# Second MLP product: halves of the columns in the order 0, 1, 1, 0, with accumulators kept over two chunks

## The chip, the cores and the metric

The kernel runs on one core of one Trainium2 chip. The metric is the device time of one execution in microseconds (us). The core has a matrix engine (TensorE, in the profile PE, with its weight loads as PEld), a vector engine (VectorE, DVE), a scalar engine (ScalarE, ACT), GpSimd (POOL) and SyncE (SP), which issues the loads. Matmuls write into eight accumulator banks of 128 x 512 float32; only ACT and DVE read these.

## What is computed

The reference is one layer of an encoder on 256 tokens with 2048 features: two kinds of attention, a cross attention and an MLP, each followed by a LayerNorm. The change lies in the MLP:

```python
ff = jnp.square(jax.nn.relu(x @ w_mlp_in)) @ w_mlp_out      # 2048 -> 8192 -> 2048
x = layer_norm(ALPHA * x + ff, ln3_g, ln3_b)
```

## The kernel before

**Precision.** Every float32 product is made of three matmuls. Each operand is split into a high part (rounded to the matmul's format by a copy on ACT, L961) and a low part (operand minus high part, on DVE, L962); high x high, high x low and low x high are added in a bank (`mm3`, L163). A split of up to 1024 columns by 128 partitions is called a part here (`part`, L964). The high parts rotate through four buffers (`w_hi`), the low parts through four fixed ones.

**The MLP's loops.** The 8192 hidden features are four chunks of sixteen column tiles of 128. Two neighbouring tiles make a pair; a chunk has eight pairs, numbered 0 to 7. A column tile ("g", `hidden_tile`, L1027) multiplies 128 columns of the first weight by all 256 tokens: two parts, 32 matmuls. After its last matmul it is evacuated (L874: a copy on ACT, an add on DVE). Once both tiles of a pair are there, the pair's stages run (`stages`, L883): relu and square on ACT, the split of the square into high and low (`halve`), and, where it is asked for, four sums and differences of its blocks (`add`, three instructions on DVE) and their split (`halve_sums`).

A unit ("u") is one pair times one half of the output columns (1024 of 2048, `q` = 0 or 1), on one 1 MB tile of the second weight. A plain unit (P) takes eight block products, so 24 matmuls of 512 columns, and two parts. A unit in seven products (S, Strassen's scheme in Winograd's form) takes 21 matmuls, four parts, three adds on DVE for sums of weight blocks (`push_sums`, L948, into `s_t`), and the pair's own sums. It accumulates in seven banks: x11, x12, x21, and p1, p5, p6, p7; x22 gets plain units only, and serves as the bank of column tiles between S units.

**The order.** `items` (L914) lists tiles and units in the order of their work. A half-pass is eight units of one chunk and one half; tiles of the coming pairs stand between. Before, each half-pass has eight tiles (none in the last), its units go 0 to 7, pairs 0 to 5 as S and 6 and 7 as P; the last half-pass has P alone. With S and P for units and g for tiles, the first two half-passes read `ggSgSgSgSgSgSgPP gSgSgSgSgSgSgPgP`. At the end of every half-pass the banks are merged into the result rows `res` on DVE: eight operations of 512 columns for p1, p5, p6, p7 (L1153, handed out between parts through the deque `banks`) and four for the x banks (L1179). The last half-pass holds back the second token block of its last four units (`HELD`), to end with few matmuls.

**What is fixed in order.** Instructions passed through `queue` (L105) keep the order in which the program emits them on their engine: all splits, all matmuls of this stage, the weight sums, LN2's row adds (`norm_ops`, L1212). The pair stages are left to the scheduler, but those of a chunk's last pair (tile 15) and of the first four tiles go through `queue` too (L1063, L1056). A pair's stages are emitted at the next tile, or after the next unit, whichever comes first (L1073, L1176). `after(n, ...)` puts work behind the n-th coming part.

**Loads.** `fetch` (L925) issues one load of 1 MB per item, some three items ahead, into four tiles in turn; `row_b`, which first holds LN2's gain and bias rows, joins as the fifth at the item `JOIN` (L923). `norm_ops(0)` and `norm_ops(1)` apply these rows to the two column halves of `res`, four operations of 1024 columns each.

Of the kernel before, what the change touches and what calls it, by code (L numbers as in the profile page):

```python
# [38 lines left out]
def encoder_kernel(ctx: ExitStack, tc: tile.TileContext, t, out):  # L39
# [798 lines left out]
    ORDER = tuple(range(CH // 2))  # L838
    SEVENS = {cq: SEVEN for cq in PASSES[:-1]}
    SEVENS[PASSES[-1]] = ()  # L840
# [7 lines left out]
    ht_x = aux[:, 0:1024].rearrange("p (k c) -> p k c", c=512)  # L848
    sums_h = [aux[:, o:o + 1024] for o in range(1024, 8192, 1024)]
# [6 lines left out]
    place, free = {}, {"h": list(range(SLOTS)), "s": list(range(len(SEVEN) + 1))}  # L856

    def take(what, c, p):
        place[what, c, p] = free[what].pop(0)
# [23 lines left out]
    def stages(h, c, p, to=free_order):  # L883

        a11, a21, a12, a22 = [h[:, o:o + P] for o in range(0, 4 * P, P)]
        s = []

        def square():
            to(nc.scalar.activation(h, h, AF.Relu))
            to(nc.scalar.activation(h, h, AF.Square))  # L890

        def halve():
            take("h", c, p)
            x = hid(c, p)
            ordered_split(x[:, :, 0:S], x[:, :, S:2 * S], h.rearrange("p (i c) -> p i c", c=S), to)

        def add():
            s.append(tmp_tile())
            s3, s1, s2, s4 = [s[0][:, o:o + P] for o in range(0, 4 * P, P)]
            to(nc.vector.tensor_tensor(out=s[0][:, 0:2 * P].rearrange("p (i c) -> p i c", c=P),  # L900
                                       in0=a21[:, None, :].broadcast_to([P, 2, P]),
                                       in1=h.rearrange("p (i c) -> p i c", c=P)[:, 0:4:3, :], op=ALU.subtract))
            to(nc.vector.tensor_tensor(out=s2, in0=s1, in1=a11, op=ALU.subtract))
            to(nc.vector.tensor_tensor(out=s4, in0=a12, in1=s2, op=ALU.add))
# [10 lines left out]
    for c, q in PASSES:  # L915
        us = [("u", c, q, p) for p in ORDER]
        gs = [("g", c, j) for j in range(LEAD, CH)] if q == 0 else [
            ("g", c + 1, j) for j in range(LEAD) if c < NCH - 1]
        for u in us:
            n = 2 if q == 0 and u[3] == (CH // 2 - 2 if c else 0) else 1  # L920
            items += gs[:n] + [u]
            gs = gs[n:]
    JOIN = items.index(("u", 0, 1, 7))  # L923

    def fetch():  # L925

# [89 lines left out]
    def both(*todo):  # L1016
        return [lambda: [x() for x in todo]]

    now, late_finish, later, count = [], [], [], [0]

    def after(n, *todo):

        later.extend([(count[0] + n, x) for x in todo])
        later.sort(key=lambda x: x[0])


    def hidden_tile(it, ps):  # L1027
# [57 lines left out]
        x = sums_of(c, p)  # L1085
        return x[:, 0, i * P:(i + 1) * P], x[:, 1, i * P:(i + 1) * P]

    def one_pass(c, q):

        order, sevens = ORDER, SEVENS[c, q]  # L1090
        final = (c, q) == PASSES[-1]
# [3 lines left out]
        left = {id(ps): len(sevens) * (ps is not x22) + 2 * (len(order) - len(sevens)) for ps in xs}  # L1095
        left.update({id(ps): len(sevens) for ps in pt})
        left[id(x22)] -= 2 * HELD * final
        total = dict(left)
# [17 lines left out]
        def more(ps, op=ALU.add):  # L1116
            nc.vector.tensor_tensor(out=m_t, in0=m_t, in1=ps, op=op)

        spare, n_seven, n_unit, parts = [], 0, 0, []
        while n_unit < len(order):  # L1120
            it = step()
            if it[0] == "g":
                if n_unit == 0:
                    ps = {LEAD: x22, LEAD + 1: x21}[it[2]] if it[1] == 0 else p6
                elif n_seven < len(sevens):
                    ps = x22
                else:
                    spare = spare or [p1, p6]
                    ps = spare[0]
                    spare.reverse()  # L1130
                hidden_tile(it, ps)
                continue
            p, raw, k = it[3], raw_of[it], 2 * it[3]
            n_unit += 1
            if p in sevens:
                if n_seven == 0:
# [10 lines left out]
                n_seven += 1  # L1147
                if at[0] < len(items) and is_seven(items[at[0]]):
                    push_sums(items[at[0]])
                if n_seven == len(sevens):  # L1150
                    nc.scalar.activation(m_t, p1, AF.Copy)

                    banks.extend([lambda: merge(r11, m_t), lambda: more(p6),  # L1153
                                  lambda: merge(r12, m_t, ALU.subtract), lambda: more(p7, ALU.subtract),
                                  lambda: merge(r21, m_t), lambda: merge(r22, m_t, ALU.subtract),
                                  lambda: merge(r22, p5), lambda: merge(r12, p5)])
            elif final and len(order) - n_unit < HELD:
                n = len(parts) // 2
# [7 lines left out]
            else:  # L1166
                for i in range(2):
# [4 lines left out]
            if q == 1:  # L1172
                give("h", c, p)
                if p in SEVEN:
                    give("s", c, p)
            if late_finish:  # L1176
                late_finish.pop()()
        if not final:
            for r, ps in ((r22, x22), (r12, x12), (r11, x11), (r21, x21)):  # L1179
                merge(r, ps)  # L1180
            if c == NCH - 1:
                xs[:], pt[:] = pt[:], xs[:]
# [36 lines left out]
    for g in range(LEAD // G):  # L1219
# [163 lines left out]
```

## Time and profile before

| | |
|---|---|
| time, median of 3 runs | 1097.58 us (1096.8 to 1098.6) |
| the profiled execution's own time | 1098.32 us |
| its span, first to last instruction | 1096.5 us |
| granted TensorE clock, mean | 0.996 |
| first column tile of the MLP's stage | 446.1 us after the start |
| last matmul | 1085.2 us |

A row of the timeline gives start, length, engine, line of the program, operation, what it writes and reads, and in brackets how long the engine was idle before it and what ended the wait. A row of a group gives count, busy time, the mean of one in ns, and the idle time before. [...]

### The profile page before, as it was taken

What the parts mean: (1) busy time and instruction counts of PE and PEld (TensorE: products, weight loads), DVE (VectorE), ACT (ScalarE), POOL (GpSimd) and SP (SyncE); (2) the same over time, 40 slices, a digit from 0 to 9 for tenths busy, and PEclk for the clock granted to TensorE, in tenths of its full rate; (3) what the DMA queues carried; (4) which work ended last, traced back from release to release, by engine and by line L of the source; (5) the groups of instructions that cost most, each with busy time, mean ns of one, the idle gap of its engine ahead of it and who ended that gap; (6) DMA issues with size and microseconds to landing.
All of it is one profiled execution on the core that took longest, in us unless ns stands there. A gap on an engine that the chain in (4) does not pass through costs nothing.

```text
span 1096.5 us, 15253 instructions
## 1 busy us (share of the span) xinstructions
PE 1076.7 (98%) x5846; PEld 928.8 (85%) x5846; DVE 938.7 (86%) x1301; ACT 642.3 (59%) x937; POOL 36.2 (3%) x43
## 2 busy tenths in 40 slices
PE   9999999999999999999999999999999999999995
PEld 6988899988999878878888888888888888888885
DVE  6878678778889677999999999899999899999876
ACT  6555567555576426656566557466566566666640
POOL 2402000000000000000000000000000000000000
PEclk9999999999999999999999999999999999999998
DMA  9664454466577334555556555646556555655732
GB/s 327 246 227 136 156 189 157 156 228 238 182 216 267 143 128 176 209 192 198 191 202 244 202 188 199 216 170 226 198 186 225 198 192 198 224 175 195 253 145 78
DMA packets 37369, 215.87 MB, mean 197 GB/s; under 512 B 4272, under 2 KB 5168, under 8 KB 13616
## 3 DMA queue, kind: packets, MB, share of 16 engines
q1 hardware_dynamic: 37296, 214.89, 55.5%
q8 instruction: 46, 0.75, 0.3%
q14 instruction: 27, 0.22, 0.1%
HBM read 212.78 MB, written 2.10 MB: 196 GB/s over the span
## 4 chain that ended last, share of the span: by engine, by line
PE 92%; DVE 6%; issue 1%; ACT 1%; DMA 1%; SPq 0%; POOL 0%; DVEq 0%; ACTq 0%
PE acc L164 12%; PE acc L165 12%; PE acc L166 12%; PE acc L1035 11%; PE att L1035 6%; PE acc L1043 6%; PE att L165 5%; PE att L166 5%; PE att L164 5%; PE att L1043 3%; PE acc L206 2%; PE acc L204 2%; PE acc L205 2%; DVE lo L962 2%; PE acc L213 1%; PE att L213 1%
## 5 line engine op out<-in xcount | busy, mean ns | idle before, releaser
L87 ACT ACTIVATE w_hi<-raw 128x1024 fp32r<-128x1024 f32 (+2 forms) x134 | 131.6, 989 | 108.5 <-PE acc L166 73.9
L88 DVE TENSOR_TENSOR w_lo<-raw,w_hi 128x1024 fp32r<-128x1024 f32 (+2 forms) x130 | 147.2, 1142 | 50.3 <-ACT w_hi L87 49.2
L962 DVE TENSOR_TENSOR lo<-raw,w_hi 128x1024 fp32r<-128x1024 f32 (+1 forms) x156 | 173.0, 1128 | 9.2 <-ACT w_hi L961 9.0
L961 ACT ACTIVATE w_hi<-raw 128x1024 fp32r<-128x1024 f32 (+1 forms) x156 | 149.3, 980 | 25.5 <-PE acc L166 15.0
L1035 PE MATMUL acc<-x2t,w_hi 128*128 128x512 f32 x592 | 153.3, 391 | 0.0
L1035 PEld LDWEIGHTS acc<-x2t,w_hi 128*128 128x128 f32 x592 | 108.9, 189 | 19.6
L962 DVE TENSOR_TENSOR lo<-s_t,w_hi 128x1024 fp32r<-128x1024 f32 x84 | 102.4, 1222 | 10.8 <-ACT w_hi L961 10.7
L961 ACT ACTIVATE w_hi<-s_t 128x1024 fp32r<-128x1024 f32 x84 | 88.6, 1057 | 37.3 <-PE acc L1035 18.4
L1043 PEld LDWEIGHTS acc<-x2t,lo 128*128 128x128 f32 x592 | 80.8, 190 | 5.8
L1043 PE MATMUL acc<-x2t,lo 128*128 128x256 f32 x592 | 82.5, 282 | 0.0
L1035 PE MATMUL att<-x2t,w_hi 128*128 128x512 f32 x304 | 78.4, 391 | 0.0
L165 PE MATMUL acc<-lo,ht 128*128 128x512 f32 (+1 forms) x188 | 73.0, 389 | 1.1 <-DVE lo L962 1.1
L164 PE MATMUL acc<-w_hi,ht 128*128 128x512 f32 x186 | 72.5, 390 | 0.0
L166 PE MATMUL acc<-w_hi,ht 128*128 128x512 f32 x186 | 72.4, 389 | 0.0
L876 ACT ACTIVATE tmp<-acc 128x256 f32<-128x256 f32 x41 | 15.4, 384 | 92.2 <-PE acc L1035 87.9
L165 PE MATMUL acc<-w_lo,xt 128*128 128x512 f32 (+2 forms) x192 | 69.3, 362 | 0.0
L166 PE MATMUL acc<-w_hi,xt 128*128 128x512 f32 (+2 forms) x192 | 69.2, 361 | 0.0
L164 PE MATMUL acc<-w_hi,xt 128*128 128x512 f32 (+2 forms) x192 | 65.6, 361 | 1.2 <-ACT w_hi L87 1.2
L1035 PEld LDWEIGHTS att<-x2t,w_hi 128*128 128x128 f32 x304 | 55.8, 189 | 10.0
L962 DVE TENSOR_TENSOR lo<-raw_x,w_hi 128x1024 fp32r<-128x1024 f32 (+1 forms) x50 | 55.4, 1124 | 0.6 <-ACT w_hi L961 0.4
L165 PE MATMUL att<-lo,aux 128*128 128x512 f32 x139 | 54.4, 391 | 1.4 <-DVE lo L962 1.4
L164 PE MATMUL att<-w_hi,aux 128*128 128x512 f32 x139 | 54.1, 390 | 0.0
(287 smaller groups left out, 2513.1 us busy)
## 6 DMA issues: line engine op xcount, KB each, us to landing
raw<-in_w_mo SPq DMA_DIRECT2D x39, 1024.0 KB, 4.8
raw<-in_w_mc SPq DMA_DIRECT2D x37, 1024.0 KB, 4.8
raw<-in_w_out SPq DMA_DIRECT2D x16, 1024.0 KB, 4.9
raw_x<-in_w_mo SPq DMA_DIRECT2D x14, 1024.0 KB, 4.8
raw_x<-in_w_mc SPq DMA_DIRECT2D x12, 1024.0 KB, 4.8
row_b<-in_w_mo SPq DMA_DIRECT2D x11, 1024.0 KB, 4.8
raw<-in_w_mi SPq DMA_DIRECT2D x8, 1024.0 KB, 4.8
row_b<-in_w_mc SPq DMA_DIRECT2D x7, 1024.0 KB, 4.8
```

Of the source, the lines that this page charges most:

```text
L87: pin(nc.scalar.activation(hi, src, AF.Copy), pinned)
L88: return pin(nc.vector.tensor_tensor(out=lo, in0=src, in1=f(hi), op=ALU.subtract), pinned)
L164: keep(nc.tensor.matmul(ps, ah, bh, start=start, stop=False))
L165: keep(nc.tensor.matmul(ps, ah, bl, start=False, stop=False))
L166: keep(nc.tensor.matmul(ps, al, bh, start=False, stop=stop))
L204: nc.tensor.matmul(ps, hi, xt[:, k, 0:S], start=k == 0, stop=False)
L205: nc.tensor.matmul(ps, hi, xt[:, k, S:2 * S], start=False, stop=False)
L206: nc.tensor.matmul(ps, lo, xt[:, k, 0:S], start=False, stop=k == nk - 1)
L961: queue(nc.scalar.activation(hi, src, AF.Copy))
L962: queue(nc.vector.tensor_tensor(out=lo, in0=src, in1=f(hi), op=ALU.subtract))
L1035: queue(nc.tensor.matmul(ps, hi[:, k * P:(k + 1) * P], x2t[:, k0 + k, :], start=k0 + k == 0, stop=k0 + k == KT - 1))
L1043: queue(nc.tensor.matmul(ps[:, 0:S], lo[:, k * P:(k + 1) * P], x2t[:, k0 + k, 0:S], start=False, stop=False))
```

## The change

The half-passes take the column halves in the order 0, 1, 1, 0, 0, 1, 1, 0 over the four chunks. Where two neighbouring half-passes have the same half, the banks stay open over both, and are merged once. So there are five groups of half-passes: the first alone, three of two, the last alone. Which unit is S or P, in which order the pairs come and how many tiles stand before each unit is written out in three tables. Half-passes 2 to 6 have six and ten tiles in turn (the first has eight, the second ten, the last none). The last tile of a chunk now stands before the unit of pair 5; the plain pair 6 and pair 7 follow without tiles, pair 7 as S in the first three chunks. With the same letters the order is:

```
ggPggSgSgSgSgSPS  ggPggPgSgSgSgSgSgS
gSgSgSgSgSgSPS    ggPggSgSgSgSgSgSgS
gSgSgSgSgSgSPS    ggPggSgSgSgSgSgSgS
gSgSgSgSgSgSPP    PSPSPPPP
```

Pair 0 of the first chunk no longer needs sums. x22 is merged on its own after a run of P that an S follows. `norm_ops(1)` moves from the second half-pass into the first parts of the first one, `JOIN` to its unit of pair 4. The hidden pairs get eight slots instead of nine, the sums eight instead of seven. In the last half-pass the banks trade places in another order, and the four held units write their low parts into slots of sums that are no longer read.

```diff
-    SEVEN = (0, 1, 2, 3, 4, 5)
-    PASSES = [(c, q) for c in range(NCH) for q in range(2)]
-    SEVENS = {cq: SEVEN for cq in PASSES[:-1]}
-    SLOTS = CH // 2 + 1
+    PASSES = [(c, (n + c) % 2) for c in range(NCH) for n in range(2)]
+    UNITS = ["PSSSSSPS", "PPSSSSSS", "SSSSSSPS", "PSSSSSSS", "SSSSSSPS", "PSSSSSSS", "SSSSSSPP", "PSPSPPPP"]
+    ORDERS = [(0, 1, 2, 3, 4, 5, 6, 7), (0, 6, 1, 2, 3, 4, 5, 7), (0, 1, 2, 3, 4, 5, 6, 7), (6, 0, 1, 2, 3, 4, 5, 7),
+              (0, 1, 2, 3, 4, 5, 6, 7), (6, 0, 1, 2, 3, 4, 5, 7), (0, 1, 2, 3, 4, 5, 6, 7), (7, 0, 6, 1, 2, 3, 4, 5)]
+    TILES = ["22111100", "22111111", "11111100", "22111111", "11111100", "22111111", "11111100", "00000000"]
+    SEVENS = {cq: [p for p, x in zip(o, u) if x == "S"] for cq, o, u in zip(PASSES, ORDERS, UNITS)}
+    SUMS = [set(SEVENS[c, 0] + SEVENS[c, 1]) for c in range(NCH)]
...
-        return [square, halve] + [add, halve_sums] * (p in SEVEN)
+        return [square, halve] + [add, halve_sums] * (p in SUMS[c])
...
-    JOIN = items.index(("u", 0, 1, 7))
+    JOIN = items.index(("u", 0, 0, 4))
...
+        c, q = PASSES[n]
+        final, units, sevens = n == len(PASSES) - 1, UNITS[n], SEVENS[c, q]
+        opens = n == 0 or PASSES[n - 1][1] != q
+        closes = final or PASSES[n + 1][1] != q
...
+        def tile_bank(it):
+
+            before, later_ = items[:at[0] - 1], items[at[0]:]
+            units = [x for x in before if x[0] == "u"][-1:] + [x for x in later_ if x[0] == "u"][:1]
+            if all(is_seven(x) for x in units) or it[1:] == (0, LEAD):
+                return x22
+            ahead = later_[:next(i for i, x in enumerate(later_) if is_seven(x))]
+            return p1 if sum(x[0] == "g" for x in ahead) % 2 or n == len(PASSES) - 2 else p6
...
+                    xs_done = [lambda r=r, ps=ps: merge(r, ps) for r, ps in ((r12, x12), (r11, x11), (r21, x21))]
+                    banks.extend([lambda: merge(r11, m_t), lambda: more(p6)] + xs_done * (units[-1] == "S") + [
+                        lambda: merge(r22, p5), lambda: merge(r12, p5),
+                        lambda: merge(r12, m_t, ALU.subtract), lambda: more(p7, ALU.subtract),
+                        lambda: merge(r21, m_t), lambda: merge(r22, m_t, ALU.subtract)])
...
+                if not final and n_unit < len(units) and units[n_unit] == "S":
+                    banks.append(lambda: merge(r22, x22))
...
-    for cq in PASSES:
-        if cq == (0, 1):
-            for i, x in enumerate(norm_ops(1)):
-                after(6 * i + 8, x)
-        one_pass(*cq)
+    for i, x in enumerate(norm_ops(1)):
+        after(2 * i + 6, x)
+    for n in range(len(PASSES)):
+        one_pass(n)
```

More of the change, by code (lines that the diff above doesn't have):

```diff
@@ L847, in encoder_kernel @@
     aux = big.tile([P, 8192], F32R, tag="big", name="aux")
-    ht_x = aux[:, 0:1024].rearrange("p (k c) -> p k c", c=512)
-    sums_h = [aux[:, o:o + 1024] for o in range(1024, 8192, 1024)]
+    sums_h = [aux[:, o:o + 1024] for o in range(0, 8192, 1024)]
     fixed = [late.tile([P, 1024], F32R, name=f"lo{i}") for i in range(4)]
@@ L854, in encoder_kernel @@
     fixed_lo.extend(fixed)
-    place, free = {}, {"h": list(range(SLOTS)), "s": list(range(len(SEVEN) + 1))}
+    place, free = {}, {"h": list(range(CH // 2)), "s": list(range(len(sums_h)))}
     def take(what, c, p):
@@ L909, in halve_sums @@
             ordered_split(y[:, 0, :], y[:, 1, :], s[0], to)
-        return [square, halve] + [add, halve_sums] * (p in SEVEN)
+        return [square, halve] + [add, halve_sums] * (p in SUMS[c])
     raws, raw_of, fetched, sums = [raw_x], {}, [0], deque()
     items = []
[L915 to L922, printed above, removed]
-    JOIN = items.index(("u", 0, 1, 7))
+    tiles = [("g", c, j) for c in range(NCH) for j in range(CH)][LEAD:]
+    for (c, q), order, counts in zip(PASSES, ORDERS, TILES):
+        for p, n in zip(order, counts):
+            items += [tiles.pop(0) for _ in range(int(n))] + [("u", c, q, p)]
+    JOIN = items.index(("u", 0, 0, 4))
     def fetch():
@@ L1014, in hidden_group @@
         return [lambda i=i, h=h: empty(i, h) for i, h in pairs], todo
-    def both(*todo):
-        return [lambda: [x() for x in todo]]
-    now, late_finish, later, count = [], [], [], [0]
+    now, late_finish, later, count, held_lo = [], [], [], [0], []
     def after(n, *todo):
@@ L1051, in hidden_tile @@
         if first:
-            after(4, lambda: evacuate(ps, h, j % 2, queue))
+            after(3 if j in (LEAD, LEAD + 2) else 4, lambda: evacuate(ps, h, j % 2, queue))
         else:
@@ L1094, in one_pass @@
         (x11, x12, x21, x22), (p1, p5, p6, p7) = xs, pt
[L1095 to L1098, printed above, removed]
+        if opens:
+            cols = [slice((2 * q + i) * 512, (2 * q + i + 1) * 512) for i in range(2)]
+            r11, r12, r21, r22 = run["res"] = [res[b][:, cc] for b in range(NB) for cc in cols]
+            whole = units if closes else units + UNITS[n + 1]
+            n_s, n_p = whole.count("S"), whole.count("P")
+            run["left"] = {id(ps): n_s + 2 * n_p for ps in (x11, x12, x21)}
+            run["left"].update({id(ps): n_s for ps in pt})
+            run["left"][id(x22)] = 2 * (n_p - HELD) * final
+            run["total"] = dict(run["left"])
+            run["fresh"] = [r11, r12, r21, r22] if c == 0 else []
+            run["s"] = run["sevens"] = n_s
+        r11, r12, r21, r22 = run["res"]
+        left, total, fresh = run["left"], run["total"], run["fresh"]
         def mm(ps, x, hi, lo):
@@ L1103, in mm @@
             mm3(ps, *x, hi, lo, start, left[id(ps)] == 0, queue)
-        cols = [slice((2 * q + i) * 512, (2 * q + i + 1) * 512) for i in range(2)]
-        r11, r12, r21, r22 = [res[b][:, cc] for b in range(NB) for cc in cols]
-        fresh = [r11, r12, r21, r22] if c == 0 else []
         def merge(r, x, op=ALU.add):
@@ L1117, in more @@
             nc.vector.tensor_tensor(out=m_t, in0=m_t, in1=ps, op=op)
-        spare, n_seven, n_unit, parts = [], 0, 0, []
-        while n_unit < len(order):
+        def tile_bank(it):
[5 more added lines that the diff above has]
+            return p1 if sum(x[0] == "g" for x in ahead) % 2 or n == len(PASSES) - 2 else p6
+        n_unit, parts = 0, []
+        while n_unit < len(units):
             it = step()
             if it[0] == "g":
[L1123 to L1131, printed above, removed]
+                hidden_tile(it, tile_bank(it))
                 continue
@@ L1135, in one_pass @@
             if p in sevens:
-                if n_seven == 0:
+                if run["s"] == run["sevens"] and not final:
                     while banks:
@@ L1166, in one_pass @@
             else:
+                if left[id(x22)] == 0:
+                    rest = units[n_unit - 1:]
+                    left[id(x22)] = total[id(x22)] = 2 * (len(rest) - len(rest.lstrip("P")))
                 for i in range(2):
@@ L1178, in one_pass @@
         if not final:
[L1179 to L1182, printed above, removed]
+            if closes and units[-1] == "P":
+                for r, ps in ((r22, x22), (r12, x12), (r11, x11), (r21, x21)):
+                    merge(r, ps)
+            if n == len(PASSES) - 2:
+                xs[:], pt[:] = [p1, p6, p7, p5], [x11, x12, x21, x22]
                 banks.extend([lambda b=b, r=r: stats(sts[b], r)
                               for b, r in ((0, r11), (0, r12), (1, r21), (1, r22))])
+                used = [place["s", c, p] for p in SEVENS[PASSES[-1]]]
+                held_lo[:] = [i for i in range(len(sums_h)) if i not in used] + used
             return
@@ L1226, in encoder_kernel @@
             rows = norm_ops(0)
-            (a1, a2, a3, a4), (b1, b2, b3, b4) = first, second
-            side.extend(wait * 4 + empty + [a1, b1, a3, a2, a4, b3] + both(b2, rows[0])
-                        + both(b4, rows[1]) + rows[2:])
+            (a1, a2), (b1, b2, b3, b4) = first, second
+            side.extend(wait * 4 + empty + [a1, b1, a2, b3, b2, b4] + rows)
             s_in.split, s_in.beside = queued_split, 2
```

29 lines of the change are left out of this document (11 added, 18 removed).

## The prediction

> **What bounds the kernel now.** The page's first part and the chain of waits come first:
>
> ```profile
> PE 1076.7 (98%) x5846; PEld 928.8 (85%) x5846; DVE 938.7 (86%) x1301; ACT 642.3 (59%) x937; POOL 36.2 (3%) x43
> ...
> PE 92%; DVE 6%; issue 1%; ACT 1%; DMA 1%; SPq 0%; POOL 0%; DVEq 0%; ACTq 0%
> ```
>
> PE sets the time; DVE holds 6% of the chain. A busy PE isn't a PE at full pace, so I read the pace from the timeline of PE, by the first matmul (L1035) of column tiles. (S is a unit in seven products, P a plain one, g a column tile.)
>
> ```profile
> 598.77 1.98 PE L1035 MATMUL att<-x2t,w_hi 128*128 128x512 f32 x8
> 609.80 1.98 PE L1035 MATMUL att<-x2t,w_hi 128*128 128x512 f32 x8
> 631.17 1.98 PE L1035 MATMUL acc<-x2t,w_hi 128*128 128x512 f32 x8
> 641.52 1.75 PE L1035 MATMUL acc<-x2t,w_hi 128*128 128x512 f32 x7
> ```
>
> One g with a P takes 609.80 - 598.77 = 11.03 us, one g with an S 10.35. The 0.68 between them are three matmuls (24 against 21), so one costs 0.227, an S 21 x 0.227 = 4.8, a P 5.45 and a g what is left, 5.6. Against this pace two stretches lose time:
>
> ```profile
> 462.04 1.98 PE L1035 MATMUL acc<-x2t,w_hi 128*128 128x512 f32 x8
> 497.54 1.98 PE L1035 MATMUL acc<-x2t,w_hi 128*128 128x512 f32 x8
> ...
> 545.05 1.98 PE L1035 MATMUL acc<-x2t,w_hi 128*128 128x512 f32 x8
> 588.42 1.98 PE L1035 MATMUL acc<-x2t,w_hi 128*128 128x512 f32 x8
> ```
>
> Three steps of g and S: 35.50 instead of 31.05, 4.45 lost (stages left over from the first groups of tiles). Four steps: 43.37 instead of 41.40, 1.97 lost (the four adds of LN2's rows, L1215, fall there). The windows by stretch show what stands behind:
>
> ```profile
> 446.00:498.00 52.00, 48.99 (x249) 40.40 (x247) 49.89 (x69) 36.42 (x52) 0.00 (x0) 1.00 0.57 203
> 683.00:767.00 84.00, 84.00 (x431) 71.90 (x430) 77.09 (x95) 51.83 (x68) 0.00 (x0) 1.00 0.57 201
> 767.00:851.00 84.00, 84.00 (x431) 71.85 (x431) 79.61 (x103) 53.08 (x70) 0.00 (x0) 1.00 0.56 200
> 1040.00:1086.00 46.00, 45.48 (x224) 38.46 (x222) 32.21 (x45) 12.94 (x14) 0.91 (x1) 1.00 0.33 124
> ```
>
> After a stretch's length stand PE, its weight loads, DVE, ACT and POOL, then the granted clock. From 683 on PE never stops, with DVE at 92 to 95% behind it. DVE has room only in the last pass (32 of 46).
>
> **What the change removes.** The unit strings hold 48 S and 16 P, where before 42 and 22 stood; 56 tiles stay. Six units lose three matmuls each: 18 x 0.227 = **4.1 us** less.
>
> **What DVE gets.** Prices from the groups by line, and spacing from DVE's timeline:
>
> ```profile
> L962 DVE TENSOR_TENSOR lo<-raw,w_hi 128x1024 fp32r<-128x1024 f32 x129 | 156.5, 1220 | 9.2 <-ACT w_hi L961 9.0
> L877 DVE TENSOR_TENSOR tmp<-acc,tmp 128x256 f32<-128x256 f32 x41 | 17.0, 421 | 7.0 <-ACT tmp L876 6.8
> ...
> 680.83 0.68 DVE L1114 TENSOR_TENSOR res<-res,m_t 128x512 f32<-128x512 f32 x1
> 681.43 2.35 DVE L962 TENSOR_TENSOR lo<-raw,w_hi 128x1024 fp32r<-128x1024 f32 x2
> ```
>
> Back to back, 1024 wide takes 2.35 - 1.22 = 1.13, 512 wide 0.60; I put 256 wide at 0.34. An S: three wide lo, one narrow, sums of 1.13 + 2 x 0.60: 6.3. A P: 2.3. A tile: 2 x 1.13 + 0.34 = 2.6, and half of a pair's stages (halving 0.6, sums 0.74 + 0.6): 1.0. So g with S costs DVE 9.9 of PE's 10.35, in runs of twelve steps now instead of six. Six more S cost 6 x 4.0 = 24 us. Against it stand the merges: twelve of 0.60 in each of seven half-passes before (50 us); now eleven in each of four groups, some eight of x22 alone, and eight more in the last pass, 60 in all (36 us). Over 600 us DVE gets about 12 more with two added sum stages: 2%, within its room on average. I cost it at nothing in the runs, with PE's matmuls as cover; without that cover it is the rival below.
>
> **The beginning.** P leads the first half-pass and two tiles stand before it and after it. Up to the fourth S, PE gets a P and two tiles more (16.6), DVE 2.3 + 2 x 2.6 and the four row adds of 4.5 that move there (12.0). The 4.6 of room is about the 4.45 lost; but the stages of pairs 4 and 5 still fall together, beside S2. I leave 1.5 of it (0 to 3). The second half has no row adds, so 1.97 goes. JOIN, the first weight load into row_b, moves 20 items forward, to the twelfth; on SP it stands behind three loads issued ahead, and the adds that it waits for are over by S1. I cost it at nothing; a late one would hold every load behind it. Together: -6.4 + 1.5 = **-4.9**.
>
> **The end of a chunk.** Here I expect the cost. The last tile (15) comes before S5, then P6 without tile, then S7 (half-passes 0, 2, 4). The rest of pair 7 (square, halve, sums) is still put into the fixed order (queue) after S5's four parts, so P6's split stands behind it on ACT and on DVE. Before, the order was tile 15, P6, rest, P7:
>
> ```profile
> 694.25 0.38 ACT L876 ACTIVATE tmp<-att 128x256 f32<-128x256 f32 x1 [4.25 <-PE att L1035]
> 695.13 0.63 ACT L889 ACTIVATE tmp<-tmp 128x512 f32<-128x512 f32 x1 [0.49 <-DVE tmp L877]
> 695.79 0.63 ACT L890 ACTIVATE tmp<-tmp 128x512 f32<-128x512 f32 x1
> 696.46 0.63 ACT L880 ACTIVATE ht<-tmp 128x512 fp32r<-128x512 f32 x1
> 697.00 1.99 ACT L961 ACTIVATE w_hi<-raw 128x1024 fp32r<-128x1024 f32 x2
> ...
> 697.12 0.69 DVE L881 TENSOR_TENSOR ht<-tmp,ht 128x512 fp32r<-128x512 f32 x1 [2.03 <-ACT ht L880]
> 698.08 2.36 DVE L962 TENSOR_TENSOR lo<-raw,w_hi 128x1024 fp32r<-128x1024 f32 x2 [0.26 <-ACT w_hi L961]
> ```
>
> ACT stood idle for 4.25 us until the tile ended, since the rest was queued ahead of P7's split; P6 on PE (5.45) hid it. The rest's three steps on ACT start 0.66 apart. Now the last S of a half-pass before, for the timing of S5 (the last four rows are from an earlier pair's sums):
>
> ```profile
> 762.25 0.40 PE L164 MATMUL att<-w_hi,ht 128*128 128x512 f32 x1
> 767.04 1.98 PE L1035 MATMUL att<-x2t,w_hi 128*128 128x512 f32 x8
> ...
> 762.45 0.39 ACT L876 ACTIVATE tmp<-acc 128x256 f32<-128x256 f32 x1 [2.64 <-PE acc L1035]
> 762.74 1.05 ACT L961 ACTIVATE w_hi<-s_t 128x1024 fp32r<-128x1024 f32 x1
> ...
> 763.82 1.23 DVE L962 TENSOR_TENSOR lo<-s_t,w_hi 128x1024 fp32r<-128x1024 f32 x1 [0.52 <-ACT w_hi L961]
> ...
> 436.40 0.29 DVE L903 TENSOR_TENSOR tmp<-tmp 128x128 f32<-128x128 f32 x1
> 436.73 0.29 DVE L904 TENSOR_TENSOR tmp<-tmp 128x128 f32<-128x128 f32 x1
> ...
> 437.05 0.63 ACT L880 ACTIVATE aux<-tmp 128x512 fp32r<-128x512 f32 x1 [1.23 <-DVE tmp L904]
> 437.59 1.04 ACT L961 ACTIVATE w_hi<-raw 128x1024 fp32r<-128x1024 f32 x1
> ```
>
> I call the tile's end, where the S starts, 0 (762.25). The last part's w_hi runs from 0.5 to 1.5 on ACT; PE ends the S at 4.8 (767.04) and wants P6's first lo one matmul later, at 5.0. The rest then goes: relu from 1.45, square 2.1, halving's hi 2.8 to 3.4; on DVE halving's lo 3.4 to 4.0, then the three adds, 0.45, 0.33 and 0.3 apart, to 5.1 (L903 and L904 above); sums' hi on ACT 5.1 to 5.75, P6's w_hi from 5.65 (0.54 after it, as at 437) to 6.7, its lo to 7.95. PE stands for 2.9, with 0.1 to start again: **3.0 us**, three times, **+9.0**. It can't go below nothing; at most another 0.5 each, if the evacuation of tile 15 is late. Behind P6 the S7 has what it needs: two parts of P6 (2.3), three adds (2.3) and four lo (4.0) are 8.6 of DVE in PE's 10.3. In half-pass 6 pair 7 has no sums: P6's w_hi starts at 3.35, its lo ends at 5.65, the copy of p1 adds 0.5 on ACT: **+0.9** (0.6 to 1.5).
>
> **The last pass** runs P, S, P, S and four held P. From P6 of half-pass 6 to its second S, DVE is asked for four P (9.2), two S (12.6), 12 merges (7.2), 4 statistics (2.4) and 0.6: 32.0, PE for 31.4, after a start 0.9 late. I take **+1.1** (0 to 3): statistics may slide to the end, where DVE has room.
>
> **The clock.** One earlier gap is on record:
>
> ```profile
> 395.29 0.66 PE L752 MATMUL att<-ident,res 128*128 128x128 f32 x4 [0.72 <-DVE res L740]
> 397.51 2.04 PE L213 MATMUL acc<-x2t,wide 128*128 128x512 f32 x4 [1.57 <-ACT x2t L757]
> ...
> 396.00:398.00 2.00, 0.48 (x1) 0.50 (x2) 1.43 (x3) 1.35 (x3) 0.00 (x0) 0.81 0.00 0
> 398.00:400.00 2.00, 2.00 (x8) 1.63 (x6) 1.85 (x5) 0.50 (x1) 0.00 (x0) 0.50 0.00 0
> 400.00:402.00 2.00, 2.00 (x12) 1.77 (x12) 0.97 (x2) 0.06 (x1) 0.00 (x0) 0.83 0.00 0
> ```
>
> After 0.72 and 1.57 us of idle PE the granted clock is 0.81, 0.50 and 0.83 in three windows: 0.4 + 1.0 + 0.3 = 1.7 us lost. The 4.45 us lost in pieces between 446 and 498 left it at 1.00 (window above). A gap of 2.9 lies beyond the 2.3 that brought the drop, but each of these stands alone, with full PE on both sides. I count one drop in the three, **+1.7** (0 to 5.1). [...]
>
> **The sum.** -4.1 - 4.9 + 9.0 + 0.9 + 1.1 + 1.7 = +3.7. The profiled execution took 1098.32 (span 1096.5 and 1.8 around it): 1102.0. The median of the runs shown is 1097.58, 0.74 lower: **1101.3**, of itself from 1098.5 to 1105.
>
> **The rivals.** (1) The pair's rest doesn't stop P6. The point is 5.0 us after the tile's end: a first lo of P6 by then costs nothing, and 9.9 and the clock's 1.7 go: 1101.3 - 11.6 = **1089.7**, faster. For it: P6's w_hi has a free buffer by then, and ACT is idle 41% of the span. Against: the fixed order, which the 4.25 us of idle ACT show. 0.17. (2) The stop is half as long, 1.5 each, without a drop of the clock: 1101.3 - 4.5 - 1.7 = **1095.1**, if stages overlap where I set them end to end. 0.15. (3) The clock stays full through every stop, as it did from 446 to 498: 1101.3 - 1.7 = **1099.6**. 0.15. [...] (4) DVE becomes the bound in the twelvefold runs: over 36 steps, 9.9 of 10.35 leaves 0.45; gaps for ACT's hi of 0.65 a step would cost 0.2 x 36 = 7: **1108**. Against it: the full windows above, where such runs of six lose nothing. 0.07. (5) The banks kept open, or eight hidden slots instead of nine, make a halving wait for PE and give the saving back without these stops: about **1097**. 0.03. The forecast itself: 0.43.
>
> Same means within 0.2%, about what a measurement of this kernel can tell from no change: 1095.4 to 1099.8. Slower: 0.39 of the forecast, 0.07 of (3), 0.07 of (4): 0.53. Faster: (1) and half of (2), 0.24. Same: what is left, 0.23. The range takes in most of (1)'s side and stops short of (4): **1090 to 1105.5**; the bound for three drops of the clock lies inside it.
>
> **What would show it.** In half-passes 0, 2 and 4: PE idle for about 3 us ahead of P6, waiting for w_hi (L961) and lo (L962); on ACT relu, square and two hi in a row between S5's last w_hi and P6's first. No loss left in the second half of chunk 0. 18 fewer matmuls of 512. If PE passes from S5 to P6 without a gap, the sum is wrong by its largest term; if g with S takes over 10.35 in the long runs, DVE was underpriced.

## The result: 1.8% slower, with most of it in six stops of TensorE

| | before | after |
|---|---|---|
| median (us) | 1097.58 | 1117.18 (1114.96 to 1118.03) |
| ratio, 95% interval | | 1.0176 [1.0162, 1.019] |
| profiled execution / its span (us) | 1098.32 / 1096.5 | 1117.34 / 1115.5 |
| mean granted clock of the profiled execution | 0.996 | 0.984 |

The forecast was 1101.3 with a range to 1105.5. The sign was right, the size was not: 15.9 us are missing. In this part lines are those of the kernel after: the split of a part, L961 and L962 before, is L957 (high, ACT) and L958 (low, DVE); the weight sums are L950, a column tile's matmuls L1028 and L1036, the merges L1114 and L1115, the additions into `m_t` L1118 and the copy of p1 L1153. L876 and L877 (eviction of a tile), L880 and L881 (split of the pair's stages), L889 and L890 (relu, square) and L900 to L904 (the pair's adds) keep their numbers.

The page's first part and the chain of waits, after:

```profile
PE 1083.9 (97%) x5828; PEld 935.0 (84%) x5828; DVE 954.0 (86%) x1315; ACT 653.8 (59%) x949; POOL 34.8 (3%) x43
...
PE 91%; DVE 6%; ACT 1%; issue 1%; DMA 0%; POOL 0%; DVEq 0%; SPq 0%; ACTq 0%
```

The page hardly differs: 18 matmuls fewer, and yet PE is busy 7 us longer, which points to matmuls that ran slower. The stage begins at the same time in both (446.11 before, 446.08 after), so the whole difference lies behind that. The table of what PE waits for, from 440 us to the end, has four rows, ten waits:

```profile
PE acc L165 <- DVE lo L958: 6.5, 5, 2.6
PE acc L164 <- ACT w_hi L957: 5.4, 3, 1.8
PE att L1028 <- DVE m_t L1118: 3.3, 1, 3.3
PE att L165 <- DVE lo L958: 1.4, 1, 1.4
```

(After the colon: us in total, times, longest.) Three waits for w_hi of the same 1.8 us, as many as there are half-passes with P6 behind S5 and ahead of S7; one for `m_t`, on which no step of the prediction counts. Where nothing of this falls, PE runs through. Windows by stretch (length; PE, weight loads, DVE, ACT, POOL; granted clock; then the DMA engines' share and GB/s):

```profile
552.00:700.00 148.00, 148.00 (x765) 126.92 (x764) 132.00 (x163) 93.68 (x122) 0.00 (x0) 1.00 0.55 197
716.00:872.00 156.00, 156.00 (x808) 133.84 (x807) 147.85 (x184) 99.85 (x130) 0.00 (x0) 1.00 0.56 197
888.00:1040.00 152.00, 152.00 (x786) 130.42 (x785) 144.42 (x181) 98.47 (x127) 0.00 (x0) 1.00 0.55 196
```

So the twelvefold runs lose nothing, with DVE at 86 to 95% (132.00 of 148, 147.85 of 156) behind them. All of the loss lies outside these windows. I added it up from the starts of PE's matmuls (a row of one 512 wide is 0.39 long, and the next starts 0.23 after it: 521.41 and 521.63 in after): what a step takes beyond 0.227 us (512 wide) or 0.120 (256 wide) is a stop, or, where a whole row of matmuls is stretched alike, the half clock (a granted clock of 0.50).

| place in after | at us | stop | half clock behind it | forecast of the stop |
|---|---|---|---|---|
| A: second S of half-pass 0 | 485.6 | 4.83 | 1.08 | 1.5 |
| B: S5 to P6, half-pass 0 | 525.7 | 3.12 | 0 | 3.0 |
| C: first tile of half-pass 1 | 539.1 | 3.79 | 2.35 | none |
| D: S5 to P6, half-pass 2 | 702.6 | 3.37 | 2.65 | 3.0 |
| E: S5 to P6, half-pass 4 | 875.5 | 3.12 | 1.59 | 3.0 |
| F: S5 to P6, half-pass 6 | 1047.2 | 1.98 | 1.69 | 0.9 |
| sum | | 20.2 | 9.4 | |

The same sum over the stage before gives 6.3. With 18 x 0.227 = 4.1 for the matmuls that went: -4.1 - 6.3 + 20.2 + 9.4 = +19.2, and the two profiled executions stand 19.0 apart. Only 0.2 is left over. (Of the stops of A, C and D some 0.25 each is the first matmul behind the stop, which already ran at half clock; without it D's is 3.12, as B's and E's.)

**B, D and E are what the prediction drew.** The timeline of after at B, ACT then DVE then PE:

```profile
521.65 1.05 ACT L957 ACTIVATE w_hi<-s_t 128x1024 fp32r<-128x1024 f32 x1
522.60 0.62 ACT L889 ACTIVATE tmp<-tmp 128x512 f32<-128x512 f32 x1
523.25 0.63 ACT L890 ACTIVATE tmp<-tmp 128x512 f32<-128x512 f32 x1
523.91 0.63 ACT L880 ACTIVATE ht<-tmp 128x512 fp32r<-128x512 f32 x1
526.29 0.63 ACT L880 ACTIVATE aux<-tmp 128x512 fp32r<-128x512 f32 x1 [1.75 <-DVE tmp L904]
526.83 3.46 ACT L957 ACTIVATE w_hi<-raw 128x1024 fp32r<-128x1024 f32 x4
...
525.97 0.29 DVE L904 TENSOR_TENSOR tmp<-tmp 128x128 f32<-128x128 f32 x1
526.96 0.69 DVE L881 TENSOR_TENSOR aux<-tmp,aux 128x512 fp32r<-128x512 f32 x1 [0.69 <-ACT aux L880]
527.90 1.23 DVE L958 TENSOR_TENSOR lo<-raw,w_hi 128x1024 fp32r<-128x1024 f32 x1 [0.25 <-ACT w_hi L957]
...
525.73 0.39 PE L166 MATMUL acc<-w_hi,ht 128*128 128x512 f32 x1
527.92 0.50 PE L164 MATMUL acc<-w_hi,ht 128*128 128x512 f32 x1 [1.81 <-ACT w_hi L957]
529.18 0.50 PE L165 MATMUL acc<-lo,ht 128*128 128x512 f32 x1 [0.76 <-DVE lo L958]
```

The reader is to see relu, square and two hi between S5's last w_hi (521.65) and P6's first (526.83), ACT idle for 1.75 us in the midst of them for DVE's adds, and PE passing 525.73 with nothing to do. S5 starts at 521.17, and P6's first lo is there at 529.13: 7.96 after it, where 7.95 was worked out. PE's two steps take 2.19 and 1.26 instead of 0.227 each: 3.0 us of stop, 3.1 with the step behind it, which takes 0.34 (529.18 to 529.52).

**C was not seen.** DVE and PE of after at the first tile of half-pass 1:

```profile
541.91 0.68 DVE L1118 TENSOR_TENSOR m_t<-m_t,att 128x512 f32<-128x512 f32 x1
...
539.07 0.39 PE L166 MATMUL acc<-w_hi,ht 128*128 128x512 f32 x1
542.74 1.62 PE L1028 MATMUL att<-x2t,w_hi 128*128 128x512 f32 x3 [3.29 <-DVE m_t L1118]
```

`tile_bank` alternates p1 and p6, counted backwards from the next S. Half-pass 1 reads `gg P gg P g S`: five tiles stand ahead of the S, so p6 falls to the first of them. p6 is free only when DVE has added it into `m_t` (541.91 to 542.59), in a queue of splits and merges; p1 is free as soon as ACT has copied it (L1153, 535.75 to 536.33).

**A is larger than I left it, and F too.** At A, DVE, ACT and PE of after:

```profile
483.46 0.42 DVE L900 TENSOR_TENSOR tmp<-tmp 128x256 f32<-128x256 f32 x1
484.81 0.42 DVE L877 TENSOR_TENSOR tmp<-acc,tmp 128x256 f32<-128x256 f32 x1 [0.94 <-ACT tmp L876]
485.15 0.28 DVE L903 TENSOR_TENSOR tmp<-tmp 128x128 f32<-128x128 f32 x1
...
484.40 0.38 ACT L876 ACTIVATE tmp<-acc 128x256 f32<-128x256 f32 x1 [2.07 <-PE acc L1028]
...
488.61 0.50 PE L165 MATMUL acc<-lo,ht 128*128 128x512 f32 x1 [2.65 <-DVE lo L958]
```

The eviction of tile 12 (L876, L877) isn't fixed in order; the scheduler put it between a pair's first add and its second. ACT waits 2.07 us for that tile's end and DVE 0.94, with the rest of pairs 4 and 5 behind them.

At F, DVE of after:

```profile
1045.91 1.28 DVE L1115 TENSOR_TENSOR res<-res,att 128x512 f32<-128x512 f32 x2
1047.11 0.68 DVE L881 TENSOR_TENSOR ht<-tmp,ht 128x512 fp32r<-128x512 f32 x1
1047.71 0.68 DVE L1118 TENSOR_TENSOR m_t<-m_t,att 128x512 f32<-128x512 f32 x1
1048.31 2.35 DVE L958 TENSOR_TENSOR lo<-raw,w_hi 128x1024 fp32r<-128x1024 f32 x2
```

The closing group is merged here, among the work that P6 waits for: two merges stand ahead of the pair's lo, and the addition at 1047.71 lies between the pair's lo and P6's and puts P6's off by 0.60.

### The profile page after: what moved, and what is told of

Read it like the earlier page. It is cut to its first block, busy times and chain, and to the rows that moved or that the text cites. A ratio compares the mean times of both kernels' runs of the same rounds, so it can differ in the third digit from the quotient of the medians.

```text
span 1115.5 us, 15269 instructions
## 1 busy us (share of the span) xinstructions
PE 1083.9 (97%) x5828; PEld 935.0 (84%) x5828; DVE 954.0 (86%) x1315; ACT 653.8 (59%) x949; POOL 34.8 (3%) x43
## 4 chain that ended last, share of the span: by engine, by line
PE 91%; DVE 6%; ACT 1%; issue 1%; DMA 0%; POOL 0%; DVEq 0%; SPq 0%; ACTq 0%
PE acc L1028 13%; PE acc L165 12%; PE acc L164 12%; PE acc L166 12%; PE acc L1036 7%; PE att L1028 5%; PE att L165 4%; PE att L166 4%; PE att L164 4%; PE att L1036 3%; PE acc L206 2%; PE acc L204 2%; PE acc L205 2%; PE acc L213 1%; PE att L213 1%; DVE lo L958 1%
## 5 line engine op out<-in xcount | busy, mean ns | idle before, releaser
L958 DVE TENSOR_TENSOR lo<-raw,w_hi 128x1024 fp32r<-128x1024 f32 (+1 forms) x150 | 163.5, 1108 | 7.9 <-ACT w_hi L957 7.7
L1028 PE MATMUL acc<-x2t,w_hi 128*128 128x512 f32 x640 | 165.9, 391 | 0.0
L957 ACT ACTIVATE w_hi<-raw 128x1024 fp32r<-128x1024 f32 (+1 forms) x150 | 141.6, 965 | 17.3 <-PE acc L166 8.4
L958 DVE TENSOR_TENSOR lo<-s_t,w_hi 128x1024 fp32r<-128x1024 f32 x96 | 117.1, 1221 | 22.4 <-ACT w_hi L957 22.4
L1028 PEld LDWEIGHTS acc<-x2t,w_hi 128*128 128x128 f32 x640 | 117.8, 189 | 21.2
L957 ACT ACTIVATE w_hi<-s_t 128x1024 fp32r<-128x1024 f32 x96 | 101.4, 1057 | 56.6 <-DVE lo L958 13.5
L1036 PEld LDWEIGHTS acc<-x2t,lo 128*128 128x128 f32 x640 | 87.3, 190 | 6.2
L1036 PE MATMUL acc<-x2t,lo 128*128 128x256 f32 x640 | 89.2, 282 | 0.0
L876 ACT ACTIVATE tmp<-acc 128x256 f32<-128x256 f32 x44 | 16.6, 386 | 108.7 <-PE acc L1028 104.4
L165 PE MATMUL acc<-lo,ht 128*128 128x512 f32 x174 | 70.9, 408 | 6.5 <-DVE lo L958 6.5
L1028 PE MATMUL att<-x2t,w_hi 128*128 128x512 f32 x256 | 67.4, 400 | 3.3 <-DVE m_t L1118 3.3
L1028 PEld LDWEIGHTS att<-x2t,w_hi 128*128 128x128 f32 x256 | 47.9, 194 | 12.3 <-issue 3.7
L164 PE MATMUL att<-w_hi,aux 128*128 128x512 f32 x140 | 54.9, 392 | 0.0
L166 PE MATMUL att<-w_hi,aux 128*128 128x512 f32 x140 | 54.9, 392 | 0.0
```

The costliest lines, as they stand in the source:

```text
L164: keep(nc.tensor.matmul(ps, ah, bh, start=start, stop=False))
L165: keep(nc.tensor.matmul(ps, ah, bl, start=False, stop=False))
L166: keep(nc.tensor.matmul(ps, al, bh, start=False, stop=stop))
L957: queue(nc.scalar.activation(hi, src, AF.Copy))
L958: queue(nc.vector.tensor_tensor(out=lo, in0=src, in1=f(hi), op=ALU.subtract))
L1028: queue(nc.tensor.matmul(ps, hi[:, k * P:(k + 1) * P], x2t[:, k0 + k, :], start=k0 + k == 0, stop=k0 + k == KT - 1))
```

## The experiments

The edits are small against the kernel after, and most take one place of the table. Two theories to begin with. **Theory A**: the six places are six separate orders of work, and each can be removed alone. **Theory B**: DVE is the bound (up to 95% in the long windows), and what is removed in one place comes up in another. Of the eleven kernels the medians are compared with runs of the kernel before on the same chip.

### The rest of pair 7 behind P6

```diff
-            if late_finish:
+            if late_finish and not (n % 2 == 0 and p == 5):
                 late_finish.pop()()
```

> The rest of pair 7 is emitted behind unit P6 instead of behind S5, in half-passes 0, 2, 4 and 6. Theory A (fixed order: P6's split stands behind the rest): the stops of 3.1 us ahead of P6 at 526, 703 and 876 us and the one of 2.0 at 1047 vanish, and with them the half-clock windows that follow (4.2 us in the first three, 1.7 in the last): 1117.2 - 9.6 - 4.2 - 3.7 = 1099.7, between 1099 and 1105. Theory B (DVE is short as a whole, the stop only shows where): the loss comes back ahead of S7 or in the long runs, 1112 or more.

Measured: 1106.93 us, ratio 1.0075 [1.0057, 1.0093]. The stops of B, D and E are gone and F went from 1.98 to 0.89; the sum of the losses falls from 29.6 to 19.2. But each of the three left a smaller stop, of 1.80, ahead of S7. DVE and PE of this version there:

```profile
706.11 0.69 DVE L1115 TENSOR_TENSOR res<-res,acc 128x512 f32<-128x512 f32 x1 [0.67 <-PE acc L166]
706.72 0.69 DVE L881 TENSOR_TENSOR aux<-tmp,aux 128x512 fp32r<-128x512 f32 x1
707.32 0.69 DVE L950 TENSOR_TENSOR s_t<-s_t,raw 128x512 f32<-128x512 f32 x1
707.92 1.82 DVE L958 TENSOR_TENSOR lo<-raw,w_hi 128x1024 fp32r<-128x1024 f32 x2
...
709.20 0.50 PE L165 MATMUL att<-lo,ht 128*128 128x512 f32 x1 [1.52 <-DVE lo L958]
```

DVE has the rest, a merge of x22 and the weight sums all ahead of S7's first lo. The mechanism of the prediction is shown by this run (take the rest away from P6, and P6 doesn't wait); the median was expected lower, since I had S7 free.

### The stop filled with matmuls

Eleven matmuls of constants into x22 ahead of P6 in half-passes 0, 2 and 4. They do no part of the computation and are overwritten.

```diff
+                for _ in range(11 * (n in (0, 2, 4) and p == 6)):
+                    queue(nc.tensor.matmul(x22, ones, ones[:, None, :].broadcast_to([P, 4, P]), start=True, stop=True))
```

> Eleven matmuls of constants into the idle bank x22 stand ahead of P6's in half-passes 0, 2 and 4; P6's first matmul overwrites them. The wait for the split stays. If the half-clock windows after the stops come from the idle PE and cost their full length: those at 705 and 879 us are gone, 4.2 us less, 1113.0; P6's second matmul still starts 7.9 to 8.0 us after S5's first. If the windows cost nothing because DVE sets the pace behind a stop: 1117.

Measured: 1112.77 us, ratio 1.0130 [1.0114, 1.0147]. PE waits as long for P6's parts as before, but does something meanwhile, and no half clock follows at D or E (nor at B, where none followed before). The windows by stretch of this version:

```profile
700.00:712.00 12.00, 11.55 (x52) 8.28 (x51) 10.95 (x15) 6.92 (x9) 0.00 (x0) 1.00 0.35 103
870.00:882.00 12.00, 11.55 (x52) 8.27 (x51) 10.95 (x15) 6.88 (x9) 0.00 (x0) 1.00 0.33 103
```

The granted clock is 1.00 in both, where the same two places of after had a stretch at half clock (0.73 over 700 to 712 us, 0.83 over 874 to 884). So the 4.2 us behind D and E in the table (2.65 and 1.59) are a second cost of the stop, and not of what PE does after it: the wait is the same, and what is gone is most of PE's idle time.

### The first tile of half-pass 1 in p1

```diff
+            if n == 1 and it[2] < 4:
+                return (p1, p6)[it[2] % 2]
             return p1 if sum(x[0] == "g" for x in ahead) % 2 or n == len(PASSES) - 2 else p6
```

> The first four tiles of half-pass 1 use p1, p6, p1, p6 instead of p6, p1, p6, p1. Theory A (the stop at 539 us waits for p6 to be emptied, p1 is free after one copy): the stop of 3.8 us and its two half-clock windows (2.4) vanish, 1111.0. Theory B (DVE is behind there anyway): the wait moves to the split of the same tile or to the next one, 1115 or more.

Measured: 1109.95 us, ratio 1.0107 [1.0086, 1.0128]. The wait for `m_t` is gone from the table of waits, and C with it: 6.1 us in the trace (3.79 and 2.35 of half clock) for one bank chosen wrongly, as expected. The medians stand 7.2 apart, since half clock also fell differently elsewhere: this trace has one stretch more of it (3.41 us) behind each of A, B and E, and none behind D.

### Pair 5's stages four parts later

```diff
-            n = 11 if j == LEAD + 1 else 5
+            n = 11 if j == LEAD + 1 else 9
```

> The stages of pair 5 of the first chunk come four parts later, so no longer together with those of pair 4. If the two pairs' stages side by side in front of S2's third part make the stop at 485 to 491 us (4.8 and 1.1 for the clock): 2 us of it stay, 1113. If the row adds of LN2 that moved there make it: 1116 to 1118.

Measured: 1112.42 us, ratio 1.0138 [1.0116, 1.0161]. A falls from 4.83 to 2.63, with 1.34 of half clock behind it: 1.9 us less in all, where 3.9 were expected. That the median still came out near 1113 is luck: in this trace half clock takes 1.6 us less behind D and 1.6 less behind E, at stops that this edit doesn't touch.

### The three together

The first, third and fourth edit in one kernel.

> The edits of e1, e3 and e4 together. Theory A (each loss is a stop of its own on PE, and what is left adds up): 18 matmuls less (-4.1), the stops of before gone (-6.3), left over are about 2.6 and 1.3 for the clock beside S2, three stops of 1.8 ahead of S7, 0.9 and 0.6 at the end: 1097.6 - 10.4 + 10.8 = 1098.0. Theory B (DVE as a whole is short): what is taken away in one place comes back in another, 1104 or more.

Measured: 1098.63 us, ratio 1.0005 [0.9996, 1.0014]. The parts add up, and theory B falls but for the 1.80 ahead of S7: with B to E mended, and A and F in part, DVE has the same work in less time. What is left of the loss in its trace: A 2.63 (and 1.32 of half clock), three times 1.80 ahead of S7, 0.89 and 0.61 in the last two half-passes: 11.1 with the small ones, against 6.3 before. The change's 4.1 of matmuls saved is still given back.

### The row adds later, alone and on top of the three

To find what is left of A: LN2's row adds go to half-pass 1, at every second part, and row_b joins the loads later.

```diff
-    JOIN = items.index(("u", 0, 0, 4))
+    JOIN = items.index(("u", 0, 1, 3))
...
-    for i, x in enumerate(norm_ops(1)):
-        after(2 * i + 6, x)
     for n in range(len(PASSES)):
+        for i, x in enumerate(norm_ops(1) * (n == 1)):
+            after(2 * i + 1, x)
         one_pass(n)
```

> As e5, and LN2's second row adds stand in half-pass 1, at its parts 1, 3, 5 and 7, with the load into row_b moved behind them. The stop beside S2 falls from 3.9 to about 1 since DVE has 4.5 us less to do there, and the two P of half-pass 1 cover the adds: 1095. If the adds cost as much in their new place: 1098.

> The changed kernel with LN2's second row adds in half-pass 1 and nothing else. If half of the stop beside S2 is theirs: 5.9 falls to about 2 there, but two adds stand ahead of the emptying of p6 and lengthen that stop by 1 to 2: 1115. If the stop is made by the pairs' stages alone: 1117 to 1119.

Measured: on top of the three 1098.62 us, ratio 1.0005 [0.9996, 1.0014]; alone on the kernel after 1117.85, ratio 1.0179 [1.0163, 1.0194]. Neither gained what the row adds were thought to cost: A is 3.07 with 1.11 more at 496.9 in the first, and 4.83 again in the second, whose C grows from 3.79 to 4.95, since one of the adds, of 1024 columns, now stands ahead of the addition into `m_t`. The row adds do not make A. Of the two reasons that I had for A, pair stages and row adds, the second falls.

### The pair's sums ahead of its halving

For the 1.80 ahead of S7, on top of the version with the row adds later: the rest in the order square, add, halve, halve_sums.

```diff
-                for stage in stages(h, c, j // 2, queue if j == CH - 1 else free_order):
+                todo = stages(h, c, j // 2, queue if j == CH - 1 else free_order)
+                for stage in todo[:1] + todo[2:3] + todo[1:2] + todo[3:] if j == CH - 1 else todo:
```

> As e6, and in the rest of a chunk's last pair the sums are added before the square is split, so that ACT and DVE wait less for each other. The three stops of 1.8 ahead of S7 fall to about 0.4: 1091, and faster than both kernels. If DVE's work alone sets these stops (8.3 us of it between the last split of S5 and the first of S7): 1.2 each stay, 1093.5.

Measured: 1098.60 us, ratio 1.0005 [0.9996, 1.0014]; the three stops are 1.81 each, and both expectations were too low. In this order too the whole rest stands behind P6's last part, and the order within it changes nothing that S7 waits for.

### Tiles 12 and 13 evicted through the queue

The traces of all versions up to here, the kernel before among them, have the eviction of tile 12 between two adds of a pair. Through `queue`, four parts later, it can't stand there. First on the kernel before:

```diff
-        if first:
+        if first or c == 0 and j in (LEAD + 4, LEAD + 5):
             after(4, lambda: evacuate(ps, h, j % 2, queue))
```

> The kernel before with one edit: tiles 12 and 13 of chunk 0 are written out and split through the queue, four parts after they are asked for, where before they were written out in free order. In the trace of before the eviction of tile 12 (L876 on ScalarE, L877 on VectorE) stands among the adds of a pair, and both engines wait for the end of that tile on TensorE (2.71 us at 490.57 and 1.06 us at 490.98); TensorE then stands still for 2.4 us at 491.8. Theory A (the eviction standing too early in the engines' order makes the stop): the stop goes, about 1095 us, 0.2% faster. Theory B (the adds of the pair itself are too much for the place): the stop stays or moves, 1097.6 us.

and the same edit on the kernel after:

> The kernel after with the same one edit: tiles 12 and 13 of chunk 0 are written out through the queue. Theory A (the eviction of tile 12 among the pair's adds makes the 4.8 us stop at 485.6, with 1.1 us of half clock behind it): about 5 us of 5.9 go, 1112.5 us. Theory B (pairs 4 and 5 fall together here, and their adds alone are too much): 1117 us.

Measured: on before 1096.68 us, ratio 0.9982 [0.9973, 0.9991]; on after 1114.18, ratio 1.0149 [1.0135, 1.0163]. The order on ACT and DVE in the kernel before:

```profile
490.98 0.42 DVE L877 TENSOR_TENSOR tmp<-acc,tmp 128x256 f32<-128x256 f32 x1 [1.06 <-ACT tmp L876]
491.32 0.28 DVE L903 TENSOR_TENSOR tmp<-tmp 128x128 f32<-128x128 f32 x1
...
490.57 0.38 ACT L876 ACTIVATE tmp<-acc 128x256 f32<-128x256 f32 x1 [2.71 <-PE acc L1035]
```

and in its edited version:

```profile
491.17 2.35 DVE L962 TENSOR_TENSOR lo<-s_t,w_hi 128x1024 fp32r<-128x1024 f32 x2
493.45 0.41 DVE L877 TENSOR_TENSOR tmp<-acc,tmp 128x256 f32<-128x256 f32 x1
...
491.92 0.36 ACT L876 ACTIVATE tmp<-acc 128x256 f32<-128x256 f32 x1
```

The eviction's rows have no wait in brackets any more, and the stop at 491 falls from 2.38 to 1.02 us. On after A falls from 4.83 to 3.32, with 1.59 of half clock. Both expectations were too large: the eviction is worth about 1.4 us of stop in each kernel. On after the rest of A is pair 5 falling beside pair 4 (2.2, from the fourth edit); with both edits, and the row adds later, the next version has 0.9 and 1.4 there.

### The best version: the rest in two pieces

The version with the row adds later, the queued eviction, and the rest of a chunk's last pair divided: square and add behind P6's first part, both splits behind P6.

```diff
+            if j == CH - 1:
+                todo = stages(h, c, j // 2, queue)
+                ahead_.append(lambda: [x() for x in todo[:1] + todo[2:3]])
+                late_finish[-1] = lambda: [x() for x in todo[1:2] + todo[3:]]
...
                             mm(to[b], a(c, k + i, b), hi, lo)
+                    if ahead_:
+                        ahead_.pop()()
```

> The row-adds version (e6) with tiles 12 and 13 of chunk 0 written out through the queue, and the rest of a chunk's last pair in two pieces: square and add behind the first part of the plain unit, the split of the sums behind the plain unit. Theory A (each remaining stop is one engine's order in that place): the stop beside the second unit goes from 4.2 to about 1 us, the three stops ahead of the last unit of seven from 1.8 to about 0.5 us each: about 1091 us, 0.6% faster than before. Theory B (the engines have no room there whatever the order): the stops move by a place and the time stays at 1098 us.

Measured: 1094.36 us, ratio 0.9968 [0.9955, 0.998], the fastest of all. DVE of this version at the place of D:

```profile
690.06 0.42 DVE L900 TENSOR_TENSOR tmp<-tmp 128x256 f32<-128x256 f32 x1
...
691.04 1.22 DVE L958 TENSOR_TENSOR lo<-raw,w_hi 128x1024 fp32r<-128x1024 f32 x1
...
693.38 0.68 DVE L881 TENSOR_TENSOR aux<-tmp,aux 128x512 fp32r<-128x512 f32 x1
```

The adds now stand between P6's two halves and run while P6 keeps PE busy; the stops of S7 come to 0.71 in each of the three half-passes (0.44 ahead of it, the rest ahead of its second part). The beginning still loses 0.91 and 1.42, where I had expected 1 together, the last two half-passes 0.88 and 0.87, so 1091 was too low. All losses of its stage come to 6.2 us, as many as before the change (6.3), and what remains of the change is what it saves in matmuls: 18 x 0.227 = 4.1, and 1098.48 - 1094.36 = 4.1. But the queued eviction helps the order before as well (1096.68): with it in both, the new order is 1096.68 - 1094.36 = 2.3 us faster.

## Why the prediction was right or wrong

The table holds the terms of the sum against the trace of after.

| term | forecast | measured |
|---|---|---|
| 18 matmuls | -4.1 | -4.1 |
| the beginning | -4.9 | -6.3 + 4.8 = -1.5 |
| end of a chunk, three times | +9.0 | +9.6 |
| first tile of half-pass 1 | not there | +3.8 |
| half-pass 6 | +0.9 | +2.0 |
| last pass | +1.1 | 0 |
| clock | +1.7 | +9.4 |

**Right.** What I expected the cost to be, P6 behind the rest of pair 7, holds to a tenth or two (B, D, E: 3.12 each without the clock's share, where 3.0 was forecast), and the rest moved behind P6 takes it away. So rivals (1), no stop, and (2), a stop half as long, are out. DVE isn't the bound of the twelvefold runs: three windows of some 150 us in which PE never stops; rival (4) is out. The 1.97 us that the second half of chunk 0 lost is gone, and no wait of PE, ACT or DVE for a load shows in the stage, so JOIN costs nothing. The sign "No loss left in the second half of chunk 0" failed all the same, since C stands there.

**Wrong in size: the clock.** "I count one drop in the three" was the step that failed, for 7.7 of the 15.9 us. At the ends of chunks it was two drops of three, the first of them twice as long as I had counted: 0 + 2.65 + 1.59 = 4.2, inside the 5.1 that I gave as a bound. The other 5.1 stand behind A, C and F, where I had no long stop and so counted none. The 1.7 rested on a single drop, at 397 us of before: the same waits at 395 us, in code that no version changes, were followed by half clock in three of the thirteen traces (before, after and the row adds alone; granted clock of 0.76 over 395 to 402 us) and in ten were not (1.00). How large the term comes out is thus in part chance, and 9.4 is what it took in one execution. Rival (3), a clock that stays full, is out: the filled stop (second experiment) shows what goes if PE isn't idle.

**Wrong by a step not made: C**, 3.8 us, and 2.35 of what the clock took. I costed the merges against DVE's room on average ("I cost it at nothing in the runs, with PE's matmuls as cover") and asked what each engine gets, but not which bank each tile takes and when it is given back. Rival (5) did name the open banks, but as a halving that waits for PE, not as a tile that waits for DVE, and put the result at 1097. The third experiment shows that the bank was all of it.

**Wrong in size: the beginning**, 3.4 us. "I leave 1.5 of it" was a remainder by feel, after DVE's room over four S (4.6) had been set against the loss (4.45). That two numbers agree showed nothing. The two smaller stops of before (1.1 and 0.9) did go; the third is a matter of order, which room on average doesn't take away. The row adds, which were counted against the room, had no part in A (two runs); an eviction worth 1.4 us of stop, visible in the trace of before as 2.71 us of idle ACT at 490.57, had, and so had pair 5 beside pair 4 (2.2).

**Half-pass 6** has 1.1 more than forecast, since merges and an addition into `m_t` stand ahead of P6's lo. **The last pass** has 1.1 less, but not because its statistics slide to the end, as the forecast allowed: four of the nine stand in its midst.

```profile
1062.61 0.68 DVE L524 BATCH_NORM_STATS2 bn<-res 128x6 f32<-128x512 f32 x1
1065.00 1.87 DVE L524 BATCH_NORM_STATS2 bn<-res 128x6 f32<-128x512 f32 x3
```

More likely F and its half clock, 3.7 us of PE, gave DVE the time: in the five versions in which F is 0.9, the last pass loses 0.6 to 0.9. No run tests this alone. That the two terms cancel is luck.

## What to carry to other kernels

A change of order is priced place by place: for each engine, what is queued ahead of the next thing that PE needs, and for each bank, which instruction frees it for its first use in the new order. An average of 90% busy told nothing of the six stops here, and was no bound either. The six stops here, of 1.98 to 4.83 us, cost from nothing to 2.65 us more each through the clock, so mending a stop can save more than its length, and shortening it too: in the first experiment 1.80 each ahead of S7 in place of 3.1 ahead of P6, with no half clock behind any of the three.

## What the runs showed of the hardware

**Half clock came in stretches of 3.41 us.** The windows of after, cut at the times at which the trace has the clock change:

```profile
398.24:401.65 3.41, 3.41 (x13) 2.91 (x12) 2.46 (x6) 0.56 (x1) 0.00 (x0) 0.50 0.00 0
490.40:493.81 3.41, 2.86 (x7) 2.28 (x8) 3.41 (x4) 1.73 (x3) 0.00 (x0) 0.50 0.65 264
527.90:531.30 3.40, 2.62 (x10) 1.96 (x11) 3.40 (x3) 2.39 (x3) 0.00 (x0) 1.00 0.02 5
541.60:548.43 6.83, 5.69 (x18) 4.86 (x19) 6.76 (x10) 1.06 (x1) 0.00 (x0) 0.50 0.59 203
705.44:712.27 6.83, 6.22 (x15) 4.93 (x16) 5.85 (x7) 2.77 (x4) 0.00 (x0) 0.50 0.43 149
879.52:882.93 3.41, 3.41 (x9) 2.65 (x8) 3.38 (x5) 0.56 (x2) 0.00 (x0) 0.50 0.22 38
1050.19:1053.60 3.41, 3.41 (x10) 2.65 (x9) 3.41 (x5) 0.07 (x1) 0.00 (x0) 0.50 0.48 159
```

While the work of after runs each stretch at 0.50 is 3.41 us long, or twice that (6.83), and their starts lie 92.16, 143.36, 307.20, 481.28 and 651.95 us behind the first, which is 27, 42, 90, 141 and 191 times 3.413. The third row, behind B, stays at 1.00. The length of a stop doesn't tell by itself whether half clock follows: it did behind F's 1.98 us and not behind B's 3.12, and behind two waits of 0.72 and 1.57 at 395 us of before (0.50 from 397.25 to 400.67), but not behind the 1.80 ahead of S7 in the first experiment.

**The same stop had two prices.** In the version of after with the queued eviction the stops of B, D and E are alike to a few hundredths, and the windows of 10 us from their beginning are these:

```profile
524.00:534.00 10.00, 7.43 (x26) 5.51 (x25) 8.92 (x11) 5.06 (x6) 0.00 (x0) 0.83 0.30 109
701.00:711.00 10.00, 7.43 (x26) 5.48 (x25) 8.90 (x13) 5.05 (x6) 0.00 (x0) 0.83 0.25 88
872.00:882.00 10.00, 7.43 (x32) 5.57 (x31) 8.95 (x13) 5.06 (x6) 0.00 (x0) 1.00 0.22 67
```

PE is busy for 7.43 us in each, in the last with 32 matmuls and in the others with 26: those ran at half clock for a while. With the three of after, four of these six stops were followed by half clock (in after 1.59 us for a stretch of 3.41 at E, 2.65 for one of 6.83 at D) and two were not. B starts at 525.7 us both in after and in the version with the first tile in p1, whose edit lies behind B; its steps are alike to 0.01 us, and yet from 529.2 to 532.5 us the granted clock is 1.00 in the one and 0.50 in the other. The runs of one kernel differ as well: of the five of after the shortest (1114.96 us) has a granted clock of 0.987, the others (1117.15 to 1118.03) 0.984. What decides which of the two prices a stop has isn't shown: no run moved a stop on purpose.
